# A decoder block on one core: three more weight-sum pieces among the row blocks, two instead of five in the MLP's first product, and an even split of 32 subtractions between VectorE and GpSimd

## The chip, the cores and the metric

The kernel runs on one core of one Trainium2 chip. The metric is device time in microseconds (us) of one execution. The time to beat is the median of three runs. Besides them there is one profiled execution, from which all durations below come.

## The reference, cut to what matters

A block of 2048 tokens by 1024 channels in float32: RMS norm, one projection (queries, keys, values, gMLP inputs, gates), dilated attention and a gated MLP over chunks, two gated branch products, an output product, and a squared-ReLU MLP. The change touches the last two stages:

```python
merged = gate_a * (y_attn @ w_branch_attn) + gate_b * (y_gmlp @ w_branch_gmlp)
y = merged @ w_out
x = x + rmsnorm(y, norm_post_mix)
h = rmsnorm(x, norm_pre_mlp)
a = relu(h @ w_mlp_in)          # 2048 x 1024 by 1024 x 4096
y = (a * a) @ w_mlp_out         # 2048 x 4096 by 4096 x 1024
x = x + rmsnorm(y, norm_post_mlp)
```

## The kernel before, in words

**Precision.** Each float32 operand is split into a high part, rounded to the matmul's format, and a low part, the rest. A product is three matmuls: high by high, high by low, low by high. ScalarE mostly makes the high part; VectorE or GpSimd subtracts to get the low part. On VectorE such a split inside the MLP goes through a copy in PSUM (`staged`), so it needs ScalarE twice and then VectorE.

**The MLP's first product** (`hstep`, `hproduct`, line 1573) uses two levels of a seven-product scheme in place of eight: sums and differences of blocks of the weight and of the input are multiplied, and the products are added up in several places. The outer level has seven phases (`OUTER`): phase 0 uses block A11 of the weight, phase 1 A12, phase 2 the sum S2, phase 3 S1, phase 4 S4, phase 5 S3 and phase 6 A22. Each phase has eight steps q = 0 to 7, and each step seven inner products of six matmuls 128x512. So the stage has 7 x 8 x 7 = 392 products, and this text numbers them from 0 in the order in which TensorE takes them; phase p begins near product 56p. A product's result is read out of PSUM by ScalarE or VectorE and added to the running tiles X.

**Order of the other engines.** In the MLP, ScalarE, VectorE, GpSimd and the DMA queue of SyncE take their instructions exactly as written. After product k, what was put down with `later(k, ...)` is issued, in the order in which it was put down. Each step needs its own inner weight sums (`combine`): five GpSimd operations (lines 1410 to 1416), between ScalarE copies and VectorE reads. GpSimd also makes low parts of the input blocks (`spot`, line 1985), differences of input blocks (lines 1470, 1495), and two kinds of work that the change moves.

**Weight sums.** The phases 2 to 5 need S1 to S4, made once per column block t = 0 to 15 of the weight ("piece") and stored in `wsd`. Pieces below `W_EARLY` are made in part 2, by `w_piece`: two loads of 512 KB into two tiles that exist once, four VectorE operations, two stores issued from GpSimd's queue. The others are made inside the MLP's first product by `w_load`, `w_sum`, `w_store`: four loads, four GpSimd operations, four stores on SyncE's queue. Before, these were five pieces, with loads at products 35, 40, 45 (phase 0) and 122, 126 (phase 2).

**m5.** Phase 3 adds its product M5 into X and also stores it. Phase 5 needs X with M5 in it, phase 6 without. `m5_load` fetches M5 (two tiles of 256 KB for each half f of a step q), and `m5_sub` subtracts it from X, five products later, for the two column halves c = 0, 1.

**Part 2** (merge, `out_block`) runs over four chunks of 512 tokens in the order 2, 3, 0, 1: a merge of 8 column blocks, then four row blocks of 128 tokens. A row block is 48 matmuls; its middle calls `mid`, which lets an older row block do its transposes (`flush_older`). Engines other than TensorE are ordered by the framework here. Half pieces are started by `next_piece`: one call loads, the next one sums and stores, each behind what the engines have in their queues at that point. Calls stand at certain column blocks of the merges and after each row block of the first three chunks.

Of the kernel before, what the change touches and what calls it, by code (L numbers as in the profile page):

```python
# [42 lines left out]
def block_kernel(ctx, tc, a, out):  # L43
    nc = tc.nc
    pe, act, dve, pool, sp = nc.tensor, nc.scalar, nc.vector, nc.gpsimd, nc.sync
# [17 lines left out]
    def psum_mm(name):  # L63
        return ps.tile([P, 512], F32, name=name, tag="mm")

    def psum_aux(name):
        return ps.tile([P, 512], F32, name=name, tag=aux_tag, bufs=BANKS[aux_tag])
# [30 lines left out]
    def mm3(ps, lh, ll, rh, rl, start, stop):  # L98
        pe.matmul(ps, lh, rh, start=start, stop=False)  # L99
        pe.matmul(ps, lh, rl, start=False, stop=False)  # L100
        pe.matmul(ps, ll, rh, start=False, stop=stop)  # L101

    def rstd_of(pl, ss, n, scale, tag):

        r = pl.tile([P, n], F32, name=f"r_{tag}", tag=f"rs_r{n}")
        act.activation(r, ss, AF.Sqrt, bias=eps, scale=scale)  # L106
        v = pl.tile([P, n], F32, name=f"v_{tag}", tag=f"rs_v{n}")
        dve.tensor_scalar(v, ss, scale, EPS, op0=OP.mult, op1=OP.add)
        dve.reciprocal(r, r)  # L109
        t = pl.tile([P, n], F32, name=f"t_{tag}", tag=f"rs_t{n}")  # L110
        if n == 1:
            dve.scalar_tensor_tensor(t, r, v, r, op0=OP.mult, op1=OP.mult)  # L112
        else:
            dve.tensor_mul(t, r, r)
            dve.tensor_mul(t, t, v)
        dve.tensor_scalar(t, t, -0.5, 1.5, op0=OP.mult, op1=OP.add)  # L116
        dve.tensor_mul(r, r, t)  # L117
        return r
# [932 lines left out]
    for n in range(len(units) + 1):  # L1051
        u = None
        if n < len(units):
            g, c, j = units[n]
# [181 lines left out]
    def out_block(c, i, mg, mid):  # L1236

        t0 = c * 512 + i * P
        isl = slice(i * P, (i + 1) * P)
        xt = bot.tile([P, D], F32, name=f"xr_{c}{i}", tag="xr")  # L1240
        sp.dma_start(xt, x[t0:t0 + P, :])
        ss = sm.tile([P, 2], F32, name=f"ss_{c}{i}", tag="ss2")
        pp = [psum_mm(f"o_{c}{i}{n}") for n in range(2)]

        ks = [(n, k) for n in range(2) for k in range(KT)]
        if i == 0:
            ks.remove((0, KT - 1))
            ks.insert(2 * KT - 2, (0, KT - 1))
        for m, (n, k) in enumerate(ks):
            if m == KT:  # L1250
                mid()
            nsl = slice(n * 512, (n + 1) * 512)
            m = mg[k // 4]
            mm3(pp[n], m[:, 0, k % 4, isl], m[:, 1, k % 4, isl], wo[k][:, 0, nsl], wo[k][:, 1, nsl], k == 0, k == KT - 1)
        tt = tt_tile(c, i)
        y1 = bot.tile([P, D], F32, name=f"y1_{c}{i}", tag="y1", bufs=2)
        for n, p in enumerate(pp):
            nsl = slice(n * 512, (n + 1) * 512)
            junk = psum_aux(f"junk_{c}{i}{n}")
            act.activation(junk, p, AF.Square, accum_out=ss[:, n:n + 1])  # L1260
            dve.tensor_mul(y1[:, nsl], p, gpost[:, nsl])
        s1 = sm.tile([P, 1], F32, name=f"s1_{c}{i}", tag="s1")
        dve.tensor_add(s1, ss[:, 0:1], ss[:, 1:2])
        r = rstd_of(sm, s1, 1, 1.0 / D, f"post{c}{i}")
        dve.scalar_tensor_tensor(xt, y1, r, xt, op0=OP.mult, op1=OP.add)
        s2 = sm.tile([P, 1], F32, name=f"s2_{c}{i}", tag="s2")
        act.activation(y1, xt, AF.Square, accum_out=s2)
        pool.dma_start(x1_d[t0:t0 + P, :], xt)
        r2 = rstd_of(sm, s2, 1, 1.0 / D, f"pm{c}{i}")
        dve.scalar_tensor_tensor(y1, xt, r2, gmlp, op0=OP.mult, op1=OP.mult)  # L1270
        yield
        for k in range(0, KT, 4):
            pt = psum_aux(f"pt_{c}{i}{k}")
            for kk in range(4):
                pe.transpose(pt[:, kk * P:(kk + 1) * P], y1[:, (k + kk) * P:(k + kk + 1) * P], ident)
            act.activation(tt[:, k:k + 4], pt.rearrange("p (k t) -> p k t", k=4), AF.Copy)
            pool.dma_start(h2_d[:, k:k + 4, t0:t0 + P], tt[:, k:k + 4])
        yield
# [3 lines left out]
    def flush():  # L1282
        if last:
            next(last.pop(0))

    def flush_older():
        if len(last) > 1:
            flush()
# [18 lines left out]
    def w_piece(t):  # L1307

        w, v = (ttp.tile([P, 2, 512], F32, name=f"{n}w{t}", tag=n, bufs=1) for n in ("tq", "tr"))
        for z, n in ((v, t + NF // 2), (w, t)):  # L1310
# [9 lines left out]
        pool.dma_start(ws_d[q][:, 0:2, f], w)  # L1320
        yield

    W_EARLY = 11
    pieces = deque([w_piece(t) for t in range(W_EARLY - 2)] + [t_piece(0), t_piece(1)] +
                   [w_piece(t) for t in range(W_EARLY - 2, W_EARLY)])
    piece = []
    PIECE_AT = {2: (4, 6), 3: (1, 3, 5, 7), 0: (1, 3, 5, 7), 1: (1, 3, 5, 7)}

    def next_piece():
        with behind():  # L1330
            if piece:
                next(piece.pop(), None)
            elif pieces:
                piece.append(pieces.popleft())
                next(piece[0])

    def merge_pieces(c, dt):
        if dt in PIECE_AT[c]:
            next_piece()
# [31 lines left out]
    NQ, HQ = NF // 2, NF // 4  # L1371
# [54 lines left out]
    def sum_ha(n):  # L1426
        w = hs_[n] = ring(n, f"hs_{n}", [P, 2, 7, 256])
        yield from combine(n, w, hraw_.pop(n))
# [109 lines left out]
    def w_load(t):  # L1538

        outer_t["w", t] = [rx.tile([P, 512], F32, name=f"wt{t}{m}", tag="xs" if (t - W_EARLY) % 2 else "c1", bufs=4) for m in range(4)]  # L1540
        for m, z in enumerate(outer_t["w", t]):
# [58 lines left out]
    m5_ = {}  # L1600
# [6 lines left out]
    def m5_sub(q, f):  # L1607
        for c in range(2):
            x_ = X[2 * q + f][:, c * 512:(c + 1) * 512]
            (dve if q > 3 and not c else pool).tensor_sub(x_, x_, m5_.pop((q, f, c)))  # L1610

    def hstep(k, n, i):

# [49 lines left out]
    def tt_tile(c, i):  # L1663

        w = bot.tile([P, D], F32, name=f"tt{c}{i}", tag=f"yt{i}") if c == 1 else \
            ttp.tile([P, D], F32, name=f"tt{c}{i}", tag="tt")
        return w.rearrange("p (k t) -> p k t", t=P)

    ttp = None
    yt = load_y(2, (("pool", "pool"),) * 4 + (("act", "dve"),) * 2)  # L1670
    early_gates(2)
    mg = merge(2, yt, {}, spatial_out)
    for n, c in enumerate(chunks):
        if n:
            mg = merge(c, yt, {0: flush, 2: flush}, lambda dt: merge_pieces(c, dt))
        for i in range(4):
            b = out_block(c, i, mg, flush_older)
            next(b)
            last.append(b)
            if n < 3 and not i:  # L1680
                yt = load_y(chunks[n + 1])
                for dt, wch in ((0, 0), (0, 1), (1, 0), (1, 1), (2, 0), (2, 1), (3, 0), (3, 1)):
                    with behind():
                        load_gate(chunks[n + 1], dt, wch)
            if n < 3:
                next_piece()
            if n == 3 and i == 1:
                e2r.close()
                egx.close()
                rx = stack(e3, "rx", 1, side="right")  # L1690
                r4 = stack(e3, "r4", 1, side="right")
                for m in range(4):
                    w = r4.tile([P, 2, 512], F32R, name=f"spot{m}", tag=f"spot{m}")
                    spots.append((w[:, 0], w[:, 1]))
                for m in range(2):
                    w = [gtp.tile([P, 512], F32R, name=f"spot{4 + m}{h}", tag=f"gt{m}", bufs=3 - m) for h in range(2)]
                    spots.append(w)
                first_op(0)
                load_ha(0)
                first_op(1)  # L1700
                load_ha(1)
                first_op(2)
                for g in sum_ha(0):
                    pass
                for j in range(2):
                    for kk in range(2):
                        first_split(j, kk)
                for g in sum_ha(1):
                    pass
                for kk in range(2):  # L1710
                    first_split(2, kk)
# [234 lines left out]
    for n in range(8):  # L1946
        t = 2 + 4 * n
        for f, d, args in ((outer_load, 0, ()), (outer_sum, 4, (0,)), (outer_sum, 6, (2,)), (outer_store, 9, ())):
            later(t + d, f, n, *args)
    for n in range(NF // 2 - W_EARLY):  # L1950
        t, d0 = (35, 40, 45, 122, 126)[n], 5 + 2 * (n > 2)
        for f, d, args in ((w_load, 0, ()), (w_sum, d0, (0,)), (w_sum, d0, (1,)), (w_sum, d0 + 1, (2,)),
                           (w_sum, d0 + 2, (3,)), (w_store, d0 + 4, ())):
            later(t + d, f, W_EARLY + n, *args)
    for q in range(HQ):
        t = 7 * 5 * HQ + (20 if q < 4 else 30) + 9 * q
        for f in range(2):
            later(t + 4 * f - 5, m5_load, q, f)
            later(t + 4 * f, m5_sub, q, f)
    gfin = None  # L1960
    for k, (_, stage, n, i) in enumerate(yorder):
# [40 lines left out]
        elif i in (3, ("p", 7)):  # L2002
# [10 lines left out]
            if stage and not more:  # L2013
                f = finish(n)
# [73 lines left out]
```

## Time and profile before

| what | value |
|---|---|
| three runs | 2582.64, 2584.74, 2586.54 us (median 2584.74) |
| the profiled execution | 2587.89 us, of which the span from first to last instruction is 2586.2 us |
| mean granted TensorE clock | 0.994 |
| busy in the span | TensorE 98%, VectorE 66%, ScalarE 49%, GpSimd 54% |
| branch and output products (part 2) | about 1064 to 1401 us |
| MLP, first product | 1401 to 1960 us |
| MLP, second product | 1950 to 2576 us |

In the rows below, PE is TensorE's matmuls, PEld its weight loads, DVE is VectorE, ACT ScalarE, POOL GpSimd, SP the queue of SyncE; L1573 is line 1573 of the kernel. A windows row gives a stretch in us from the span's start, its length, then for PE, PEld, DVE, ACT and POOL the busy time with the number of instructions that were running in the stretch, then the granted clock as a share of full speed, the busy share of the DMA engines and GB/s. A row of waits gives who waited for whom, the total in us, the number of times and the longest. A row of grouped instructions ends with busy us, mean ns, and idle time before them. A timeline row gives start, duration, engine, line, operation, and in brackets the idle time before it and who ended it.

### The profile page before, as it was taken

What the parts mean: (1) busy time and instruction counts of PE and PEld (TensorE: products, weight loads), DVE (VectorE), ACT (ScalarE), POOL (GpSimd) and SP (SyncE); (2) the same over time, 40 slices, a digit from 0 to 9 for tenths busy, and PEclk for the clock granted to TensorE, in tenths of its full rate; (3) what the DMA queues carried; (4) which work ended last, traced back from release to release, by engine and by line L of the source; (5) the groups of instructions that cost most, each with busy time, mean ns of one, the idle gap of its engine ahead of it and who ended that gap; (6) DMA issues with size and microseconds to landing.
All of it is one profiled execution on the core that took longest, in us unless ns stands there. A gap on an engine that the chain in (4) does not pass through costs nothing. (4 is left out here: it accounts for less than half of the span.)

```text
span 2586.2 us, 36297 instructions
## 1 busy us (share of the span) xinstructions
PE 2546.1 (98%) x12122; PEld 2125.5 (82%) x12122; DVE 1695.6 (66%) x3063; ACT 1271.9 (49%) x2696; POOL 1385.4 (54%) x1385
## 2 busy tenths in 40 slices
PE   9999999999999999999999999999999999999998
PEld 8888888888888887788887788888778888888886
DVE  5676575445443447777767678778787777767766
ACT  5213211154446434544445645665447776766755
POOL 0363354274545555311113858787887767767634
PEclk9999999999999999999999999999999999999999
DMA  8779778989897899877766766467884222122235
GB/s 313 284 246 325 254 244 278 308 246 296 264 329 218 239 287 326 279 263 266 272 225 240 249 204 212 145 194 215 259 258 143 90 90 89 51 90 90 90 125 201
DMA packets 413293, 568.73 MB, mean 220 GB/s; under 512 B 58929, under 2 KB 247601, under 8 KB 412082
## 3 DMA queue, kind: packets, MB, share of 16 engines
q1 hardware_dynamic: 387600, 504.73, 59.8%
q0 software_dynamic: 15616, 55.06, 5.6%
q10 hardware_dynamic: 9890, 6.62, 0.8%
q8 instruction: 96, 1.57, 0.3%
q14 instruction: 91, 0.75, 0.1%
HBM read 362.16 MB, written 204.14 MB: 219 GB/s over the span
## 5 line engine op out<-in xcount | busy, mean ns | idle before, releaser
L1573 PE MATMUL ha<-spot,hs 128*128 128x512 f32 x1344 | 327.7, 393 | 8.9 <-ACT hs L1351 2.4
L1883 PE MATMUL ya<-spot,s 128*128 128x512 f32 x1344 | 323.2, 389 | 0.0
L1573 PEld LDWEIGHTS ha<-spot,hs 128*128 128x128 f32 x1344 | 253.5, 189 | 65.6 <-ACT sa L1361 3.3
L1883 PEld LDWEIGHTS ya<-spot,s 128*128 128x128 f32 x1344 | 252.3, 188 | 52.3
L1351 ACT ACTIVATE hs<-hraw 128x512 fp32r<-128x512 f32 x168 | 105.0, 626 | 144.3 <-POOL hraw L1412 123.1
L1573 PE MATMUL hc<-spot,hs 128*128 128x512 f32 x672 | 171.1, 390 | 2.6 <-POOL spot L1985 1.7
L731 PE MATMUL g<-opA,spots 128*128 128x512 f32 x672 | 170.5, 398 | 1.8 <-DVE cv L763 1.8
L1883 PE MATMUL yc<-spot,s 128*128 128x512 f32 x672 | 170.5, 389 | 0.0
L731 PE MATMUL g<-opB,spots 128*128 128x512 f32 x648 | 164.0, 397 | 0.0
L1351 ACT ACTIVATE s<-sraw 128x512 fp32r<-128x512 f32 x168 | 104.2, 620 | 108.2 <-POOL sraw L1412 108.2
L1573 PEld LDWEIGHTS hc<-spot,hs 128*128 128x128 f32 x672 | 126.1, 188 | 30.0 <-POOL spot L1985 2.1
L99 PE MATMUL x<-hT_a,wq 128*128 128x512 f32 x384 | 149.7, 390 | 0.0
L101 PE MATMUL x<-hT_a,wq 128*128 128x512 f32 x384 | 149.5, 389 | 0.0
L100 PE MATMUL x<-hT_a,wq 128*128 128x512 f32 x384 | 149.5, 389 | 0.0
L1883 PEld LDWEIGHTS yc<-spot,s 128*128 128x128 f32 x672 | 126.2, 188 | 26.2
L74 ACT ACTIVATE hl<-r 128x512 fp32r<-128x512 f32 x48 | 30.4, 633 | 236.5 <-POOL r L332 89.0
L731 PEld LDWEIGHTS g<-opA,spots 128*128 128x128 f32 x672 | 121.1, 189 | 23.8 <-issue 2.2
L82 POOL TENSOR_TENSOR spots<-gr,spots 128x512 fp32r<-128x512 f32 x98 | 128.4, 1314 | 22.3 <-DMA gr<-in_w_in_dram 7.9
L1744 ACT ACTIVATE sraw<-sraw 128x1024 f32<-128x1024 f32 x128 | 133.9, 1046 | 2.4 <-DMA sraw<-sd 2.3
L731 PEld LDWEIGHTS g<-opB,spots 128*128 128x128 f32 x648 | 116.9, 189 | 21.1
L76 POOL TENSOR_SCALAR spots<-gr 128x512 fp32r<-128x512 f32 x86 | 55.4, 644 | 131.9 <-PE g L731 97.0
L981 DVE TENSOR_REDUCE o<-po 128x256 f32<-128x512 f32 x48 | 33.2, 692 | 133.9 <-PE po L980 133.9
(471 smaller groups left out, 6844.7 us busy)
## 6 DMA issues: line engine op xcount, KB each, us to landing
sraw<-sd SPq DMA_DIRECT2D x128, 256.0 KB, 3.3
qk<-hl SPq DMA_DIRECT2D x24, 1024.0 KB, 5.7
qq<-qk SPq DMA_DIRECT2D x96, 256.0 KB, 5.4
sd<-e SPq DMA_DIRECT2D x64, 256.0 KB, 3.6
hraw<-wsd SPq DMA_DIRECT2D x32, 512.0 KB, 4.6
w2r<-in_w_mlp_out_dram SPq DMA_DIRECT2D x16, 1024.0 KB, 9.2
g<-gated SPq DMA_DIRECT2D x56, 256.0 KB, 5.5
gr<-sgd SPq DMA_DIRECT2D x53, 256.0 KB, 5.0
```

The lines of the kernel that those rows point to most:

```text
L74: act.activation(hi, src, AF.Copy)
L76: pool.tensor_scalar(hi, src, 1.0, 1.0, op0=OP.mult, op1=OP.mult)
L82: (pool if lo_eng == "pool" else dve).tensor_sub(lo, src, f32(hi))
L99: pe.matmul(ps, lh, rh, start=start, stop=False)
L100: pe.matmul(ps, lh, rl, start=False, stop=False)
L101: pe.matmul(ps, ll, rh, start=False, stop=stop)
L731: pe.matmul(p, w[:, l, k], h[:, r, k], start=i in (1, 6, 5, 4) and not k and not m, stop=k == 3 and m == 2, skip_group_check=True)
L981: dve.tensor_reduce(ot[:, :, j * 64:(j + 1) * 64], po.rearrange("p (b h e) -> p b e h", b=4, h=2), axis=AX.X, op=OP.add)
L1351: act.activation(hi, src, AF.Copy)
L1573: pe.matmul(p, w[:, l, S_AT[i], kk * P:(kk + 1) * P], b[r], start=i in (1, 2, 5) and not kk and not z, stop=kk == 1 and z == 2, skip_group ...
L1744: act.activation(sraw_[n], sraw_[n], func)
L1883: pe.matmul(p, s[:, l], w[r], start=i in (1, 2, 5) and not m and not o, stop=m == 1 and o == 2, skip_group_check=True)
```

## The change

Three pieces more are made in part 2 (`W_EARLY` 14 instead of 11). Their six calls stand in the middle of the second and third row block of the first three chunks (`row_half`). The last two pieces stay in phase 0, with loads at products 35 and 42; phase 2 has none. Of the m5 subtractions, VectorE takes the half c = 0 and GpSimd the half c = 1 of every step; before, VectorE took c = 0 of steps 4 to 7 alone. Their places move: before, products 300 to 331 for steps 0 to 3 and 346 to 377 for steps 4 to 7; now 297 to 308 for steps 0 and 1, and 341 to 380 for steps 2 to 7.

```diff
-    W_EARLY = 11
+    W_EARLY = 14
...
     def m5_sub(q, f):
         for c in range(2):
             x_ = X[2 * q + f][:, c * 512:(c + 1) * 512]
-            (dve if q > 3 and not c else pool).tensor_sub(x_, x_, m5_.pop((q, f, c)))
+            (pool if c else dve).tensor_sub(x_, x_, m5_.pop((q, f, c)))
...
+    def row_half():
+        flush_older()
+        next_piece()
...
-            b = out_block(c, i, mg, flush_older)
+            b = out_block(c, i, mg, row_half if n < 3 and i in (1, 2) else flush_older)
...
     for n in range(NF // 2 - W_EARLY):
-        t, d0 = (35, 40, 45, 122, 126)[n], 5 + 2 * (n > 2)
+        t, d0 = (35, 42)[n], 5
         for f, d, args in ((w_load, 0, ()), (w_sum, d0, (0,)), (w_sum, d0, (1,)), (w_sum, d0 + 1, (2,)),
                            (w_sum, d0 + 2, (3,)), (w_store, d0 + 4, ())):
             later(t + d, f, W_EARLY + n, *args)
     for q in range(HQ):
-        t = 7 * 5 * HQ + (20 if q < 4 else 30) + 9 * q
+        t = 7 * 5 * HQ + (17 if q < 2 else 47) + 7 * q
         for f in range(2):
             later(t + 4 * f - 5, m5_load, q, f)
             later(t + 4 * f, m5_sub, q, f)
```

## Rows read from the trace of the kernel before

**Rows 1.** Windows of 100 us: part 2, MLP first product, MLP second product.
```profile
1200.00:1300.00 100.00, 100.00 (x464) 83.24 (x462) 69.30 (x148) 44.40 (x93) 17.43 (x26) 1.00 0.72 246
1800.00:1900.00 100.00, 94.67 (x407) 76.98 (x406) 72.99 (x113) 44.63 (x87) 77.25 (x80) 0.98 0.81 251
2060.00:2160.00 100.00, 100.00 (x443) 82.83 (x442) 70.06 (x107) 67.17 (x110) 75.34 (x82) 1.00 0.22 75
```

**Rows 2.** Windows closer up, MLP first product.
```profile
1470.00:1500.00 30.00, 25.96 (x105) 20.09 (x104) 18.61 (x29) 20.63 (x41) 28.37 (x29) 0.94 0.66 220
1510.00:1540.00 30.00, 30.00 (x134) 24.86 (x133) 22.48 (x35) 12.60 (x24) 16.46 (x19) 1.00 0.57 168
1605.00:1620.00 15.00, 14.52 (x63) 11.37 (x62) 12.15 (x19) 8.74 (x17) 13.72 (x15) 1.00 0.55 164
1840.00:1890.00 50.00, 44.67 (x187) 35.58 (x186) 35.11 (x55) 27.15 (x53) 48.59 (x48) 0.97 0.67 204
1900.00:1950.00 50.00, 50.00 (x223) 41.28 (x222) 44.65 (x67) 26.66 (x50) 44.03 (x44) 1.00 0.88 270
```

**Rows 3.** Windows of 10 us with waits of PE in them.
```profile
1480.00:1490.00 10.00, 8.07 (x28) 5.94 (x27) 7.23 (x12) 8.13 (x17) 9.76 (x10) 0.84 0.52 188
1880.00:1890.00 10.00, 7.53 (x32) 5.63 (x31) 4.47 (x8) 5.08 (x10) 9.61 (x11) 1.00 0.17 47
```

**Rows 4.** Windows with matmuls and weight loads of line 1573 alone.
```profile
1400.00:1477.00 77.00, 72.50 (x316) 59.09 (x317) 1.00 0.81 281
1400.00:1862.00 462.00, 451.73 (x1971) 370.24 (x1972) 1.00 0.68 219
```

**Rows 5.** Waits of PE, 1402 to 1960 us.
```profile
PE ha L1573 <- ACT hs L1351: 2.4, 1, 2.4
...
PE hc L1573 <- POOL spot L1985: 1.7, 1, 1.7
PE ha L1573 <- ACT X_y L1585: 1.4, 1, 1.4
PE ha L1573 <- POOL spot L1985: 1.3, 1, 1.3
```

**Rows 6.** Waits of ACT, 1855 to 1895 us.
```profile
ACT hs L1351 <- POOL hraw L1412: 19.3, 4, 9.1
```

**Rows 7.** Grouped instructions of POOL, 1840 to 1890 us.
```profile
L1610 POOL TENSOR_TENSOR X_yt<-X_yt,m 128x512 f32<-128x512 f32 x8 | 10.6, 1345 | 0.0
...
L1610 POOL TENSOR_TENSOR X<-X,m 128x512 f32<-128x512 f32 x4 | 5.1, 1294 | 0.0
```

**Rows 8.** Timeline of POOL from 1484 us.
```profile
1484.03 1.30 POOL L1549 TENSOR_TENSOR wt<-wt,wt 128x512 f32<-128x512 f32 x1
1485.29 1.28 POOL L1985 TENSOR_TENSOR spot<-hb,spot 128x512 fp32r<-128x512 f32 x1
```

**Rows 9.** Tile m (M5): durations min/median/max ns, waits, DMA landing.
```profile
L1610 DVE TENSOR_TENSOR X<-X,m x3: 694/1111/1174, 1897.5 to 1909.0; 128x512 f32<-128x512 f32 x3
...
L1610 DVE TENSOR_TENSOR X_y<-X_y,m x2: 911/1220/1530, 1932.2 to 1938.9; 128x512 f32<-128x512 f32 x2
...
DVE X L1610: 4.0, 2
...
DMA to landing us min/median/max: 4.3/6.1/9.2
```

**Rows 10.** Tile of the part-2 pieces: durations min/median/max ns.
```profile
L1315 DVE TENSOR_TENSOR trw<-trw x11: 681/685/692, 1114.3 to 1358.3; 128x512 f32<-128x512 f32 x11
```

**Rows 11.** Timeline of DVE and of PE, fourth row block and next merge.
```profile
1156.85 0.69 DVE L1261 TENSOR_TENSOR y<-o,gpost 128x512 f32<-128x512 f32 x1 [4.26 <-ACT junk L1260]
...
1163.49 1.29 DVE L1270 SCALAR_TENSOR_TENSOR y<-xr,r_pm,gmlp 128x1024 f32<-128x1024 f32 x1
...
1169.07 1.04 PE L1275 MATMUL pt<-ident,y 128*128 128x128 f32 x8
```

**Rows 12.** Waits of PE, 1130 to 1402 us.
```profile
PE pt L1275 <- DVE y L1270: 2.0, 1, 2.0
```

## Prediction

> **What bounds the kernel now.** I read first the windows of 100 us, then closer windows against undisturbed stretches of the same engine, then the waits of TensorE there, and last the queue of the engine that these waits lead to. TensorE is busy without a gap in part 2 and in the MLP's second product [rows 1]; only work on TensorE, or a wait of it, could move the time there, and the change adds no matmul. In the MLP's first product it is not: 1800 to 1900 us held 407 matmuls where 443 fit [rows 1]. An undisturbed 30 us hold 134 and an undisturbed 50 us 223, so 89 take 20 us, 0.225 us each [rows 2]. By that, 1470 to 1500 us lost 134 - 105 = 29 matmuls, 6.5 us (stretch A); 1605 to 1620 us should hold 134 - 15 / 0.225 = 67 and lost 4, 0.9 us (stretch B); 1840 to 1890 us lost 223 - 187 = 36, 8.1 us (stretch C). Together 15.5 us: the purse from which this change can take.
>
> Counting matmuls of line 1573, six to a product, 316 by 1477 us are 52.7 products, and 1971 by 1862 us are 328.5 [rows 4]: A is the end of phase 0 and the beginning of phase 1 (products 48 to 66), C the second half of phase 5. Both are places of the two kinds of work that the diff moves. TensorE's waits there name ScalarE and GpSimd: 2.4 us on `hs` of line 1351 and 1.7 us on `spot` in C, 1.4 us on ScalarE and 1.3 us on `spot` in A [rows 5]. ScalarE itself stood still for GpSimd's line 1412, 19.3 us in four waits, the longest 9.1 us [rows 6]: its queue is in order, so while it waits for a step's weight sums, it reads no product out of PSUM. And GpSimd was busy 28.37 of 30 us in A, 48.59 of 50 us in C [rows 2]. So the bound in A and C is GpSimd's queue.
>
> **The change part by part.**
>
> *Stretch A.* A weight sum is one GpSimd operation of 1.30 us [rows 8], four to a piece, 5.2 us. Before, they are issued after products 40, 40, 41, 42; 45, 45, 46, 47; 50, 50, 51, 52; now the third set is gone and the second stands at 47, 47, 48, 49. The `combine` of products 45 and 46 stood behind two sums of the second piece and now stands ahead of them, 2.6 us earlier; ScalarE's wait for it, and with it TensorE's 1.4 us, should go. The low part that TensorE then waited for (1.3 us) is issued after product 50. Ahead of it were two sums of the third piece, the second at 1484.03 us, and it ran from 1485.29 us, to 1486.57 us [rows 8]. With two sums fewer it ends 2.6 us earlier; but TensorE, no longer held before, comes some 2.3 us earlier too (1.4 us and smaller waits). So this wait stays, about 1.3 us. The granted clock in 1480 to 1490 us was 0.84 on the mean, with a stretch at 1.2 GHz after the three waits [rows 3]; in 1880 to 1890 us, with a wait of 1.7 us among 2.5 us of idle, it stayed at 1.00, 2.4 GHz [rows 3, 5]. I take the latter for the one wait that stays. Gain 6.5 - 1.3 = 5.2 us; bounds 6.5 (the wait goes too) and 2 (the clock falls after all: 10 us at 0.84 cost 1.6 us, and a longer wait).
>
> *Stretch B.* The two pieces of phase 2 go, 8 sums, 10.4 us of GpSimd before 1605 us, where it was busy 13.72 of 15 us [rows 2, 8]. Gain 0.9 us; bounds 0 and 0.9.
>
> *Stretch C.* Twelve of GpSimd's m5 subtractions ran in it, 10.6 + 5.1 = 15.7 us of its 48.6 [rows 7]. Now products 309 to 340 have none; GpSimd's four of steps 0 and 1 run at 297 to 308, in front of C, where eight ran (products 300 to 313). GpSimd then has some 33 of 50 us in C, and the line 1412 that ScalarE waited for comes up to 9 us earlier. Gain 8.1 us; bounds 8.1 and 4, if what I add in front of it takes half.
>
> *What it adds in front of C.* VectorE gets four subtractions within 12 products (16 us). On VectorE one took 0.69 to 1.53 us, with medians of 1.1 and 1.2 [rows 9]; I take 1.0, so 4 us, beside the differences of input blocks that fall there too. TensorE needs each PSUM bank again four products later, 5.4 us, less the product itself and VectorE's read of 0.7 us: VectorE may be some 3 us late. I take 0.7 us; bounds 0 and 3.
>
> *What it adds in phase 6.* Each engine gets 12 subtractions at products 341 to 380 instead of 8 at 346 to 377: every 3.5 products instead of 4.5. In 50 us (37 products) that is 10.6 instead of 8.2, 2.4 more; VectorE goes from 44.65 to some 47 us, GpSimd at 1.35 us each from 44.03 to 47.3 us [rows 2, 7, 9]. Tight, but not over. Behind each subtraction wait VectorE's reads of PSUM, and behind those TensorE. I take 0.8 us; bounds 0 and 4. In the rows, VectorE's subtraction took 0.69 us alone, and up to 1.53 us where GpSimd does the other half of the same tile just then [rows 9]. The Trainium skill (GPSIMD Engine Reference, section 1, Specifications) says that GpSimd shares its SBUF interfaces with VectorE and contends with VectorE instructions that have two SBUF inputs, which is what `m5_sub` issues, now always to both engines at once; the trace agrees with that. If each of VectorE's took the longest time, 10.6 x 1.53 - 8.2 x 1.0 = 8 us come on top of 44.65 in 50 us: VectorE is the bound by 2.7 us, and the sum loses 2 to 3 us more. This is inside the bound of 4.
>
> *Part 2.* Three pieces: 12 VectorE operations of 0.685 us are 8.2 us; 6 stores on GpSimd's queue; 6 loads of 512 KB on SyncE's queue [rows 10]. TensorE is full there, and VectorE has 69 of 100 us, GpSimd 17 [rows 1], so the cover is there. The sums now also stand between two row blocks' chains on VectorE. What hangs behind them is the normalised row block, which TensorE transposes later: for the fourth row block it was ready at 1164.8 us and taken at 1169.07 us, 4.3 us in hand, and before the fourth's reads VectorE stood idle for 4.26 us, which takes up 2.74 us of sums [rows 11]. The loads must wait on SyncE's queue for the stores of the piece before (the tiles exist once), and the next rows of x queue behind; these wait for the x tile's own store anyway. Without that cover, the one such wait in the trace cost 2.0 us [rows 12]. I take 0.8 us for three chunks; bounds 0 and 6. The transformed input pieces, `t_piece`, come one row block later and are read only in the fourth chunk; that costs nothing.
>
> *Sum.* 5.2 + 0.9 + 8.1 - 0.7 - 0.8 - 0.8 = 11.9 us. The profiled execution, 2587.89 us, would become 2576.0 us. It lies 3.15 us over the median of the three runs; taken from that median: 2584.74 - 11.9 = 2572.8, so 2573 us.
>
> **Rivals.** Under 0.2% (5.2 us) a measurement of this kernel can't be told from no change.
>
> *VectorE and DMA take GpSimd's place, in part.* A keeps its low clock (gain 2), C keeps half (4), the three costs come to 2 us: 2584.7 - 4 = 2581; with one of the three mended, 2578. For it: VectorE is at 89% in phase 6. Against: it is not behind in C, where it waits itself.
>
> *GpSimd wasn't it.* The waits of A and C name ScalarE as often as GpSimd [rows 5]; were ScalarE's own order the cause, no stall would move: 2585 us. Against: its waits for line 1412 [rows 6].
>
> *Slower.* Late M5 loads in phase 6. Each subtraction comes 5 products (6.8 us) after its load was issued. Loads landed in 6.1 us, at most 9.2 us; VectorE stood 4.0 us in two waits for them, 2.0 us each, and TensorE lost nothing [rows 9]. Now there are 12 pairs instead of 8, on DMA engines that were 88% busy in 1900 to 1950 us [rows 2]. It decides from about 10 us of landing, where VectorE's 3 us in hand are gone. At 11.5 us each of the 12 costs some 1.7 us: 2584.7 - 14.2 + 1.5 + 20 = 2592 us. Against: in C SyncE's queue was held up by GpSimd's backlog, and the loads then came in a bunch; without it they spread out.
>
> *Part 2 stalls.* At each of three chunks the transposes wait 2.0 us and the clock then falls once (1.6 us): 10.8 us lost instead of 0.8, 2583 us.
>
> **How the numbers follow.** The forecast, 2569 to 2577 us, has a chance of 0.62; VectorE and DMA in part 0.17; no effect 0.08; late loads 0.08; part 2 0.05. Faster by over 0.2% means under 2579.6: all of the first and two thirds of the second, with a little of the rest: 0.74. Slower is the late loads: 0.08. The remainder, 0.18, is the same. The low end of the range is the whole purse without a cost, 2584.7 - 15.5 = 2569, less 1 for the spread of runs: 2568; the high end takes the second case with all its costs: 2582.
>
> **What would show it.** In A, GpSimd with some 5 us less and one wait of TensorE left, on `spot`, at the clock of 2.4 GHz; in B none; in C 220 or more matmuls in 50 us and no long wait of ScalarE for line 1412; in phase 6 VectorE some 94% busy, and windows there still full. Wrong it would be through windows of phase 6 under 215 matmuls in 50 us, with VectorE waiting for m5's DMA, or through TensorE waiting for line 1270 in the merges of part 2.

## The result and the profile after

The changed kernel takes 2589.2 us in the median of 16 runs (2585.8 to 2600.52), the kernel before, measured beside it, 2584.28 us (2580.12 to 2588.22): a ratio of 1.0019 with a 95% interval of [1.0012, 1.0026], 4.9 us slower where 11.9 us less were forecast. The two profiled executions don't show this sum: that of after took 2586.54 us, that of before 2587.89 us. They show where the change acts.

Three starts cut the time at the two borders that matter: the last weight load of the row sums (line 551) begins part 2, the first matmul of line 1573 ends it and begins the MLP's first product, the last one ends that. Operations grouped by line, before and then after; the columns are count, min/median/max in ns, first and last start:

```profile
L551 PEld LDWEIGHTS rowsum<-wsp,ones x4: 187/188/188, 473.3 to 1052.5; 128*128 128x128 f32 x4
L1573 PE MATMUL ha<-spot,hs x1344: 387/389/662, 1401.4 to 1958.4; 128*128 128x512 f32 x192
L1573 PE MATMUL hc<-spot,hs x672: 387/389/505, 1415.5 to 1959.7; 128*128 128x512 f32 x168
```

```profile
L551 PEld LDWEIGHTS rowsum<-wsp,ones x4: 187/188/188, 471.8 to 1049.8; 128*128 128x128 f32 x4
L1573 PE MATMUL ha<-spot,hs x1344: 387/389/504, 1412.6 to 1956.9; 128*128 128x512 f32 x192
L1573 PE MATMUL hc<-spot,hs x672: 389/389/499, 1426.6 to 1958.2; 128*128 128x512 f32 x168
```

Part 2 went from 1401.4 - 1052.5 = 348.9 us to 362.8 us, 13.9 us more. The first product went from 1959.7 - 1401.4 = 558.3 us to 545.6 us, 12.7 us less. So the gain that the prediction worked out is there, and a loss of the same size stands in front of it.

The gain, in windows of stretches A, B, C and phase 6, moved by what part 2 and the stalls shift them (against [rows 2]):

```profile
1482.00:1512.00 30.00, 28.46 (x126) 23.13 (x125) 22.68 (x36) 23.14 (x46) 25.51 (x28) 1.00 0.65 216
1616.00:1631.00 15.00, 15.00 (x68) 12.43 (x67) 12.35 (x20) 7.29 (x14) 13.30 (x14) 1.00 0.14 37
1846.00:1896.00 50.00, 49.67 (x220) 40.79 (x219) 43.78 (x68) 31.01 (x60) 41.57 (x44) 1.00 0.73 222
1896.00:1946.00 50.00, 50.00 (x222) 41.39 (x221) 45.95 (x68) 25.39 (x48) 44.28 (x45) 1.00 0.89 290
```

A holds 126 matmuls instead of 105, C 220 instead of 187, B and phase 6 are full. The clock stays at 1.00, 2.4 GHz, in all four.

The loss, in the waits of TensorE in part 2, 1090 to 1412 us (against [rows 12]), and of VectorE there, 1115 to 1380 us, after; columns: us in total, times, longest:

```profile
PE b L99 <- DVE g L1211: 8.0, 3, 3.1
PE pt L1275 <- DVE y L1270: 4.5, 5, 2.0
```

```profile
DVE trw L1315 <- DMA trw<-in_w_mlp_in_dram: 23.1, 6, 5.5
DVE xr L1265 <- DMA xr<-in_x_dram: 20.9, 6, 4.4
...
DVE trw L1316 <- DMA tqw<-in_w_mlp_in_dram: 6.8, 4, 2.7
```

The 2.0 us among the waits for line 1270 is the old one. The others are new: 8.0 us for VectorE's reads of PSUM in the merges (line 1211) and 2.5 us for row blocks not normalised in time. VectorE itself stands for pieces and for rows of x; in the kernel before the same three rows, in the same window, read:

```profile
DVE trw L1315 <- DMA trw<-in_w_mlp_in_dram: 5.6, 2, 4.4
DVE trw L1316 <- DMA tqw<-in_w_mlp_in_dram: 5.0, 2, 2.7
...
DVE xr L1265 <- DMA xr<-in_x_dram: 2.6, 2, 1.6
```

How the first of them comes about, VectorE's timeline in the first chunk's first row blocks, after; in brackets the idle time and what ended it:

```profile
1122.26 0.16 DVE L108 TENSOR_SCALAR v_post<-s 128x1 f32<-128x1 f32 x1
1127.00 0.69 DVE L1315 TENSOR_TENSOR trw<-trw 128x512 f32<-128x512 f32 x1 [4.58 <-DMA trw<-in_w_mlp_in_dram]
1127.61 0.16 DVE L109 RECIPROCAL r_post<-r_post 128x1 f32<-128x1 f32 x1
...
1130.23 1.28 DVE L1265 SCALAR_TENSOR_TENSOR xr<-y,r_post,xr 128x1024 f32<-128x1024 f32 x1
...
1140.54 1.28 DVE L1265 SCALAR_TENSOR_TENSOR xr<-y,r_post,xr 128x1024 f32<-128x1024 f32 x1 [3.53 <-DMA xr<-in_x_dram]
```

The piece's sums stand between lines 108 and 109, in the middle of a row block's chain. VectorE's queue is in order: it stands 4.58 us for the piece, with the chain half done. Line 1265, which completes x, comes later, so does the store of the x tile, and as that tile exists once, the next rows of x are loaded later and VectorE waits for them, 3.53 us. In all it waits six times for x, 20.9 us; what these waits cost by themselves comes up with e8 below. In the merge behind these row blocks, VectorE then stands for the next piece in front of line 1211:

```profile
1180.18 0.69 DVE L1315 TENSOR_TENSOR trw<-trw 128x512 f32<-128x512 f32 x1 [1.98 <-DMA trw<-in_w_mlp_in_dram]
1183.38 0.69 DVE L1316 TENSOR_TENSOR trw<-tqw,trw 128x512 f32<-128x512 f32 x1 [2.50 <-DMA tqw<-in_w_mlp_in_dram]
1183.99 0.68 DVE L1211 TENSOR_TENSOR g<-g,b 128x512 f32<-128x512 f32 x1
```

TensorE, which needs that PSUM bank again, stood still with it, and in the second such merge the clock fell (window of 15 us; 40 matmuls where [rows 1] have 464 in 100 us, so 70):

```profile
1262.00:1277.00 15.00, 11.87 (x40) 9.21 (x40) 9.32 (x16) 4.65 (x9) 1.43 (x2) 0.77 0.75 279
```

Thirty matmuls of 0.2155 us are 6.5 us, 3.1 of them the wait and 3.4 the clock at its lower level, 1.2 GHz. The sum, 8.0 + 2.5 + 3.4 = 13.9 us, is what part 2 lost, but that it fits to the tenth is chance. The kernel before had a fall of the clock of its own in part 2, at the old wait of 2.0 us for line 1270; after had none at that wait (before, then after):

```profile
1380.00:1390.00 10.00, 9.30 (x38) 7.86 (x39) 6.87 (x18) 4.03 (x11) 2.11 (x3) 0.83 0.40 154
1390.00:1400.00 10.00, 8.01 (x40) 6.50 (x39) 6.77 (x15) 4.74 (x12) 2.69 (x4) 1.00 0.34 121
```

10 us at 0.83 cost 1.7 us, so these rows explain 12.2 us, and 1.7 us have no row. The whole of part 2, before and after:

```profile
1052.50:1401.40 348.90, 341.91 (x1576) 282.47 (x1574) 252.68 (x483) 160.62 (x323) 78.48 (x97) 0.99 0.71 245
1049.80:1412.60 362.80, 345.60 (x1577) 282.67 (x1575) 258.25 (x496) 160.55 (x323) 82.72 (x103) 0.99 0.72 252
```

TensorE stood 7.0 us in it before and 17.2 us after: 10.2 of the 13.9 us are idle time.

### The profile page after: what moved, and what is told of

The parts are those of the page before. It is cut to its first block, busy times and chain, and to the rows that moved or that the text cites. A ratio compares the mean times of both kernels' runs of the same rounds, so it can differ in the third digit from the quotient of the medians.

```text
span 2584.8 us, 36269 instructions
## 1 busy us (share of the span) xinstructions
PE 2542.6 (98%) x12122; PEld 2121.6 (82%) x12122; DVE 1705.8 (66%) x3083; ACT 1272.4 (49%) x2696; POOL 1368.0 (53%) x1371
```

## The experiments

Theory 1: VectorE waits in order for a piece's load, amid the chain and in the merges. Theory 2: VectorE has no room for 8 us more. Theory 3: six more loads and stores take the DMA's time. Part 2 and the first product are cut as above, from each kernel's profiled execution; these lie from 3.6 us below to 6.5 us above the medians. The kernels in which part 2 is unchanged (before, e1, e9, e10, e7) have 345.6 to 351.4 us, and the changed kernel and e2, which share one part 2, 362.8 and 368.0, so a difference of under 6 us of part 2 is not read. Kernels measured together share one set of runs of before; ratios go by that set.

| kernel | median us | ratio to before, 95% | part 2, us | first product, us |
|---|---|---|---|---|
| changed kernel | 2589.20 | 1.0019 [1.0012, 1.0026] | 362.8 | 545.6 |
| e1 m5 alone | 2579.61 | 0.9979 [0.9971, 0.9988] | 348.3 | 553.0 |
| e2 pieces alone | 2596.66 | 1.0048 [1.0033, 1.0062] | 368.0 | 551.7 |
| e9 m5, engines alone | 2580.53 | 0.9979 [0.9969, 0.9988] | 347.0 | 554.2 |
| e10 m5, places alone | 2581.28 | 0.9989 [0.9980, 0.9998] | 345.6 | 553.1 |
| e3 calls behind the rows | 2579.47 | 0.9978 [0.9967, 0.9988] | 358.7 | 545.7 |
| e4 loads amid rows left out | 2577.76 | 0.9973 [0.9964, 0.9982] | 353.8 | 545.8 |
| e8 sums amid rows left out | 2576.67 | 0.9965 [0.9953, 0.9978] | 350.2 | 547.5 |
| e6 those sums on GpSimd | 2591.49 | 1.0025 [1.0012, 1.0037] | 365.5 | 546.1 |
| e13 later in the merges | 2585.24 | 0.9989 [0.9980, 0.9998] | 362.3 | 545.6 |
| e11 both, e3 and e13 | 2569.99 | 0.9939 [0.9925, 0.9952] | 345.0 | 548.4 |
| e15 e1 and e13, no extra piece | 2576.29 | 0.9968 [0.9956, 0.9980] | 347.0 | 554.1 |
| e7 three pieces in phase 2 | 2579.70 | 0.9982 [0.9974, 0.9991] | 351.4 | 553.6 |
| e12 one piece in part 2 | 2578.42 | 0.9971 [0.9961, 0.9981] | 350.4 | 550.1 |
| e14 e11, piece at 40 | 2571.41 | 0.9954 [0.9941, 0.9967] | 343.0 | 548.0 |

**The two halves.** e1 is the kernel before with m5's two edits, e2 the changed kernel without them.

```diff
-            (dve if q > 3 and not c else pool).tensor_sub(x_, x_, m5_.pop((q, f, c)))
+            (pool if c else dve).tensor_sub(x_, x_, m5_.pop((q, f, c)))
-        t = 7 * 5 * HQ + (20 if q < 4 else 30) + 9 * q
+        t = 7 * 5 * HQ + (17 if q < 2 else 47) + 7 * q
```

> Before with the new places and engines of the m5 subtractions alone; part 2 and the five pieces of weight sums in the MLP stay. Theory 1 (late load: the changed kernel loses in part 2, because the sums amid a row block wait on VectorE for their load, and gains in the MLP as forecast): stretch C mended, A and B as before, part 2 as before: 2584.3 - 7.0 = 2577 us. Rival (C was mended because phase 2's sums went, not by m5): no change, 2584 us.

> The changed kernel with the m5 subtractions as before: only the pieces move. Theory 1: part 2 loses its 14 us, A and B give 5 to 6 back, C stays: 2584.3 + 14 - 5.5 = 2593 us. Rival (the loss of part 2 in the profile is that one execution's): 2584.3 - 5.5 = 2579 us.

m5 alone gains 0.21%, and 5.3 us in the first product, 2.6 us short of its forecast by the median; the pieces alone lose 0.48%, 3.7 us more than forecast, with a part 2 of 368.0 us. The loss belongs to the pieces.

**m5's two edits apart.** e9 takes the first of the two lines above, e10 the second.

> The kernel before, with m5's subtractions shared evenly between the two engines from the first on, at the places that they had. Of the twelve that GpSimd had in stretch C it keeps six, 7.8 us less of its 48.6 of 50. If the stall of C is GpSimd's load there, half of it or more goes: 2579 to 2581 us. If it is the places, nothing moves: 2584 us.

> The kernel before, with m5's subtractions at the new places and by the engines that they had: GpSimd does all of the first four steps' and half of the rest. Stretch C holds none of them and loses nothing; but eight of GpSimd's stand in 297 to 308, and sixteen in phase 6, 21 us of GpSimd more than the eight before over some 53 us that had 6 us free. If the load of GpSimd is what makes TensorE wait, the stall moves to phase 6 and the time is 2582 to 2590 us; if the places alone mend it, 2579 us.

Each alone gives nearly all that both give in the first product, 4.1 and 5.2 of 5.3 us: C stalled because GpSimd was full there, and six subtractions fewer were enough. The places alone didn't move the stall to phase 6: in 1893 to 1943 us GpSimd was busy 47.27 of 50 us, and TensorE held 222 matmuls. Of the sixteen subtractions that e10's forecast counts there, eight had stood there before, so GpSimd got 10.4 us more and not 21. By the whole time e10 can't be told from e1.

**What in part 2 costs it.** e3 keeps all work and traffic and moves the six extra calls from amid the row blocks to behind them. e4 keeps the places, but fills the tiles of the pieces begun behind the first and second row block instead of loading them.

```diff
-            b = out_block(c, i, mg, row_half if n < 3 and i in (1, 2) else flush_older)
+            b = out_block(c, i, mg, flush_older)
...
             if n < 3:
                 next_piece()
+                if i in (1, 2):
+                    next_piece()
```

```diff
+            if filled[0]:
+                pool.memset(z, 0.01)
+            else:
                 sp.dma_start(z.rearrange("p a c -> p (a c)"), a["w_mlp_in"][n].rearrange("p k c -> p (k c)"))
...
+                filled[0] = i in (0, 1)
                 next_piece()
+                filled[0] = False
```

> The changed kernel with the six extra calls moved from the middle of the second and third row block to the end of the same row block, so that a piece's sums come behind the row block's whole chain, a row block after its load; work and traffic are the same. Theory 1 (late load): the waits of TensorE in part 2 all but go, 2584.3 - 12.6 + 2 = 2574 us. Theory 2 (VectorE has no room for 8 us more of work in part 2): as the changed kernel, 2589 us. Theory 3 (6 MB more of DMA traffic): 2589 us.

> The changed kernel, but the pieces that are loaded after the first and second row block of the first three chunks are filled by GpSimd with a constant instead of loaded (so part of the weight is not computed with); sums, stores and their places stay. Theory 1 (late load): VectorE no longer waits in the chain, part 2 loses under 4 us: 2584.3 - 12.6 + 4 = 2576 us or less. Theory 2 (VectorE's work): 2589 us. Theory 3 (traffic): two thirds of the loss stay, 2585 us.

Both are faster than before, e4 1.8 us and e3 5.5 us short of what theory 1 gave. Theory 2 has e4 against it, which has all of VectorE's sums, and theory 3 has the time of e3, which has all transfers (its part 2 isn't told from the changed kernel's). e8 leaves the sums amid the row blocks out and keeps the loads and stores, e6 does these sums on GpSimd.

```diff
-        dve.tensor_add(a22, a21, a22)          # this one and the next three
+        if not amid[0]:                        # e8
+            dve.tensor_add(a22, a21, a22)
+        e = pool if amid[0] else dve           # e6
+        e.tensor_add(a22, a21, a22)
```

> The changed kernel without the sums of the pieces that end inside a row block (24 of VectorE's operations are left out, so these weight sums are stored as they were loaded); their loads and stores stay, the stores now waiting for the load by themselves. Theory 1 (VectorE stands in the middle of a row block's chain until a piece's load lands, and with it the x tile's store and its next load): part 2 comes to 351 to 355 us and the time to 2574 to 2578 us, though all the transfers of the change are there. Theory 3 (the six loads and stores more): part 2 stays at 361 to 363 us, 2589 us.

> The changed kernel, with every step of a piece that starts from inside a row block told to do its sums on GpSimd instead of VectorE; loads, stores, places and tiles stay as they are. Theory 1 (VectorE's queue is in order and stands for a piece's load in the middle of a row block's chain): the 4.6 us wait of VectorE amid the chain goes, the chains keep the times that they had before, and part 2 comes back from 362.8 us to about 350 to 353 us, the time to 2574 to 2577 us. Theory 3 (six more loads and six more stores take the DMA's time): nothing changes, 2589 us. A third way, found since: what hurts is that the next piece's tiles come free late, in the merge, because they exist once; GpSimd's sums take 5.2 us a piece instead of 2.7, so this would stay or grow: the waits for line 1211 in the merges stay, 2585 to 2589 us.

(One of the six pieces that end amid a row block is a `t_piece`, whose sums stay on VectorE in both: 20 operations are left out or moved, not 24.) e8 has every transfer of the change, and part 2 is back at 350.2 us: theory 3 falls for good. In it TensorE keeps one wait for line 1211, 4.2 us, in the last merge. e6 missed theory 1's number, and shows why that theory was told too narrowly. The third way of its forecast came about: TensorE's waits for line 1211 in the merges stay and grow (1090 to 1417 us):

```profile
PE b L99 <- DVE g L1211: 11.0, 5, 3.5
```

The row blocks' chains are held up in other ways. GpSimd's timeline in e6, where lines from 1315 on stand one lower, and VectorE's for the same block and the next:

```profile
1145.66 1.28 POOL L1317 TENSOR_TENSOR trw<-tqw,trw 128x512 f32<-128x512 f32 x1 [0.98 <-DMA tqw<-in_w_mlp_in_dram]
...
1149.47 2.17 POOL L1320 TENSOR_TENSOR tqw<-tqw 128x512 f32<-128x512 f32 x1
1152.05 0.73 POOL L1321 DMA_DIRECT2D wsd<-tqw  x1 [0.41 <-POOL tqw L1320]
1152.78 0.57 POOL L1268 DMA_DIRECT2D x1d<-xr  x1
```

```profile
1145.71 1.25 DVE L117 TENSOR_TENSOR r_post<-r_post,t_post 128x1 f32<-128x1 f32 x1
...
1148.52 1.97 DVE L1265 SCALAR_TENSOR_TENSOR xr<-y,r_post,xr 128x1024 f32<-128x1024 f32 x1 [1.55 <-DMA xr<-in_x_dram]
...
1162.45 1.28 DVE L1265 SCALAR_TENSOR_TENSOR xr<-y,r_post,xr 128x1024 f32<-128x1024 f32 x1 [4.62 <-DMA xr<-in_x_dram]
```

Line 1265 had x ready at 1148.52 + 1.97 = 1150.5 us, but its store stood behind the piece's sums and stores in GpSimd's queue until 1152.78 us, 2.3 us late, and VectorE stood 4.62 us for the next rows of x. The wait for a piece amid the chain was gone from VectorE, and the x tile's round (sum, store, load) was held up in another queue. Besides, VectorE's operations took longer beside GpSimd's sums: line 117 took 1.25 us instead of some 0.15 and ended with line 1317, line 1265 took 1.97 instead of 1.28. So e6 does not part these ways.

What a late round of x costs by itself is not shown. VectorE's waits for x, 1115 to 1380 us, in e1, whose part 2 is that of the kernel before, and in e8:

```profile
DVE xr L1265 <- DMA xr<-in_x_dram: 9.7, 5, 3.2
```

```profile
DVE xr L1265 <- DMA xr<-in_x_dram: 15.3, 8, 4.1
```

Both have more of them than the kernel before (2.6 us), and still a part 2 of 348.3 and 350.2 us.

**The merges.** e3 kept four waits for line 1211, 7.6 us together; VectorE stood there for the piece that the merge itself starts. In e13 the changed kernel does the sums of that piece one column block later, in e11 e3 does, in e15 e1 does.

```diff
-    PIECE_AT = {2: (4, 6), 3: (1, 3, 5, 7), 0: (1, 3, 5, 7), 1: (1, 3, 5, 7)}
+    PIECE_AT = {2: (4, 6), 3: (1, 4, 5, 7), 0: (1, 4, 5, 7), 1: (1, 4, 5, 7)}
```

> The version with the extra calls behind the row blocks, whose part 2 still took 358.7 us, with one more edit: in the merges of the last three chunks the first piece's sums are issued behind the fifth column block instead of the fourth, 4 us later, so that the load has landed when VectorE comes to them. There VectorE stood 2.2 + 2.8, 3.5 + 1.8 and 5.7 us for those loads, and TensorE 2.8, 0.8 and 3.8 us for VectorE's line 1211. Theory 1, told of the merges too: these three stalls go or shrink to under 1 us each, part 2 comes to 352 us, the time to 2573 to 2576 us. If the second piece of the merge, which now has only the time from its load to the merge's end, takes the wait over: 2579 to 2581 us.

> The changed kernel with the six calls where it has them, amid the row blocks, and with the later sums in the merges (fifth column block instead of fourth). If what hurts is mostly the merges, where TensorE stood 2.2, 3.1 and 2.7 us for line 1211 and ran 6.8 us at half clock, those go and the time is 2577 to 2580 us; the four short waits for line 1270, 2.5 us together, stay. If the wait amid the chain makes everything behind it late whatever the merges do (theory 1 in its first form), the merges' loads still land too late: TensorE keeps two or three of the waits for line 1211, and the time is 2584 to 2588 us. With the calls behind the rows and the same edit it was 2570.0 us.

> The kernel before with m5 as the change has it and the later sums in the merges, but no more pieces in part 2 than the kernel before has. It tells what of the 2570.0 us is owed to the extra pieces. m5 alone was 2579.6 us, part 2 348.3 us with one wait of 2.3 us for line 1211. If the late loads in the merges are the extra pieces' doing alone, the edit is worth 2 us here: 2577 to 2578 us, so the three pieces are worth 7 to 8 us once they don't wait. If the merges lost more than that before, it is 2573 to 2575 us and the pieces are worth 3 to 5 us.

The waits of TensorE in part 2, 1090 to 1390 us, in e3, in e11, and to 1400 us in e13:

```profile
PE b L99 <- DVE g L1211: 7.6, 4, 3.6
PE pt L1275 <- DVE y L1270: 2.0, 1, 2.0
```

```profile
PE pt L1275 <- DVE y L1270: 1.3, 1, 1.3
PE b L99 <- DVE gates L1211: 0.5, 1, 0.5
```

```profile
PE pt L1275 <- DVE y L1270: 9.6, 6, 2.7
PE b L99 <- DVE g L1211: 1.5, 2, 0.8
```

e11 has no wait for `g` of line 1211 left, and of those for line 1270 only the old one, now 1.3 us. By its median it is the fastest kernel of the study (e14 is not told from it), 0.6% under before and 3 us under the range forecast for it. It has all of VectorE's sums and all transfers of the change, so theories 2 and 3 fall with it as well. In e13 the waits for line 1211 shrink to 1.5 us, but those for line 1270 grow from 4.5 to 9.6: the chain that stood still in the row block is late at its transposes instead. So its time lies in the second range of its forecast, but not by the waits named there. e13 and e11 differ by nothing but the place of six calls: 0.9989 - 0.9939 = 0.50%, 13 us. e15 against e1 has the merge edit alone, 0.11%, which the intervals don't tell apart from nothing; and e11 against e15 has the three pieces, moved from the MLP phases to part 2: worth 0.9968 - 0.9939 = 0.29%, some 7 us, once TensorE no longer waits for them. Amid the chain, the changed kernel against e1, they cost 1.0019 - 0.9979 = 0.40%; behind the rows without the merge edit, e3 against e1, they gain nothing that the intervals show (0.01%).

**Other places.** e7 does the three pieces in phase 2 instead, e12 only one of them in part 2, behind the first chunk's rows. The lines shown hold the numbers that they change; neither has calls amid the row blocks.

```diff
-    W_EARLY = 14
+    W_EARLY = 11                                          # e7; 12 in e12
-        t, d0 = (35, 42)[n], 5
+        t, d0 = (35, 42, 118, 124, 130)[n], 5 + 2 * (n > 1)   # e7
+        t, d0 = (35, 42, 122, 126)[n], 5 + 2 * (n > 1)        # e12
```

> The changed kernel without its three more pieces in part 2: they are done in the third MLP phase instead, on GpSimd, from products 118, 124 and 130; the two pieces at 35 and 42 and m5's new places and engines stay. Part 2 should take 349 us again, as in the kernel before. Stretches A and C keep what the change gave them, 3.5 and 8 us. The third phase has twelve sums, 15.6 us of GpSimd, where the kernel before had eight and lost 0.9 us: 1 to 3 us lost. Theory 1 and its rivals all give 2573 to 2575 us; over 2578 us would say that A or C needed something else of the change, or that the third phase can't carry three pieces.

> One piece more in part 2 instead of three, its calls behind the second and third row block of the first chunk; two pieces in the third MLP phase, where the kernel before has them (products 122 and 126), two at 35 and 42, m5 as in the changed kernel. Stretches A and C as after the change, 3.5 and 8 us gained, B as before, part 2 at 349 to 352 us: 2574 to 2577 us. If each extra piece costs its share of what three cost in that version (10 us of part 2, 3.3 each) it is 2577 us; if one costs as much as three, 2582 us.

Phase 2 can't carry three: TensorE waited 3.9 us once and the clock fell, and the first product lost some 8 us against the changed kernel. e12 still had one merge wait of 2.8 us, and its time is 1.4 us over its forecast. Neither is told from e1: in e7, with a first product of 553.6 us, what A gains is given back.

**The wait left in A.** e14 is e11 with `(35, 40)` for `(35, 42)`.

> The version with the calls behind the row blocks and the later sums in the merges (2570.0 us), with the second piece of the first MLP phase at product 40 instead of 42. There one wait of TensorE was left in stretch A, 1.7 us at product 56; it stood on VectorE's line 1587, and that for the store of the piece's tile, whose buffer the first stage tile of the next phase takes over. If the store is the cause, it comes two products, 2.7 us, earlier, the wait goes, and the time is 2568 to 2569 us. If the low part (spot) that the prediction named is the cause, nothing moves, 2570 us. Against both, the piece's sums at 45 to 47 stand ahead of the combines of products 45 and 46 again, which cost 1.4 us in the kernel before: 2569 to 2571 us.

The wait for line 1587 went, the 1.4 us for the combine that the prediction had read in [rows 5] came back, and the time is that of e11 or 1.4 us more: the third way.

## Why the prediction was wrong

**The purse and stretches A, B, C: right.** 5.2 + 0.9 + 8.1 - 0.7 - 0.8 = 12.7 us were forecast for the first product, and 12.7 us is what the two profiles show. That they agree to the tenth is luck: by the windows A gained 126 - 105 = 21 matmuls, 4.7 us, and C 33, 7.4 us, 1.2 us less together than forecast, and the costs were smaller too. A kept one wait at full clock, B none, C has 220 matmuls, and ScalarE's longest wait for line 1412 there fell from 9.1 [rows 6] to 4.2 us. e9 and e10 confirm GpSimd's load as the cause in C, and e14 the combine's as one in A.

**A's remaining wait: right in size, wrong in name.** It was to be 1.3 us on `spot`; it was 1.5 us, on line 1587. VectorE's timeline:

```profile
1493.66 0.69 DVE L1587 TENSOR_TENSOR e<-X_yt,ha 128x512 f32<-128x512 f32 x1 [2.16 <-DMA wsd<-wt]
```

The stage tile of the first product of phase 1 takes over a buffer of the second piece, and waited for that piece's store.

**In front of C and phase 6: right.** TensorE lost 0.6 us at product 308 (0.7 forecast); phase 6 has 222 matmuls in 50 us with VectorE at 45.95 us. M5's loads landed in 4.0 to 8.2 us and no wait of TensorE names them, so the forecast's slower rival didn't happen. VectorE's subtractions took 0.68 to 1.84 us. The Trainium skill (GPSIMD Engine Reference, section 1, Specifications) says that GpSimd contends with VectorE instructions that have two SBUF inputs. The trace agrees: the longest of them, 1.84 us, started at 1940.23 us together with GpSimd's. Windows of phase 6 stayed full all the same.

**Part 2: the step that failed.** It was 0.8 us with an upper bound of 6, and measured 13.9. Its sum took VectorE's free time for cover and had no term for VectorE's wait for a piece's load, neither amid a row block's chain nor in the merges, where line 1211 cost 8.0 us. The kernel before already had such waits, 10.6 us in four (above). "TensorE is full there" was read from one window of 100 us; over the whole of part 2 it stood 7.0 us. Two sentences were wrong, and a third looked past something. The sums were put "between two row blocks' chains"; they stand inside the first one's. The cover was measured in work, 2.74 us of sums in an idle time of 4.26 us; what VectorE spent was a wait for a load, 4.58 us. It was set by when the tile came free (the store of the piece before was issued at 1113.14 us and landed 7.0 us later, the load was issued at 1120.11 us) and by the load's 6.8 us to landing, and not by how long the sums take. And that the rows of x "wait for the x tile's own store anyway" looked past a wait that grew, VectorE's for x from 2.6 to 20.9 us; by e8 it is open what that costs by itself. With the calls behind the rows, the merges alone are worth 0.9978 - 0.9939 = 0.39% (e3 against e11). The rival "Part 2 stalls" had a loss of 10.8 us and a chance of 0.05; it had the place, TensorE in the merges, but named line 1270, where 2.5 us were lost, and not line 1211 with 8.0.

The medians differ by 4.9 us, the profiled part 2 and first product together by 13.9 - 12.7 = 1.2 us. Single executions scatter by more than this. The changed kernel and e2, with one and the same part 2, have 365.4 us on the mean, the five kernels with the part 2 of before 348.2 us: a loss of 17.2 us by this estimate, and 17.2 - 12.7 = 4.5 us. The granted clock, too, varies from run to run: the 16 runs of the changed kernel have means from 0.992 to 0.997, and the time goes with them, by some 2 us for 0.001 (2600.52 us at 0.992, 2585.8 at 0.997). The profile of before had 0.994 and lay 3.6 us over the median of its runs, that of after had 0.996 and lay 2.7 us under. Why the clock falls in one run and not in another stays open.

## What to carry to other kernels

Work that waits for a load costs, on an in-order queue, its wait and not its duration: before inserting it, read when its load lands there, and which chain it would cut. Look for such waits in the kernel as it is, at every place where the same tiles are filled: here the merges had them as well as the row blocks, and mending one of the two was not enough. Where an engine has room, place such work where a chain ends and as late as the next use allows: the same three pieces cost 0.40% amid the chain, change nothing behind it, and gain 0.29% behind it with the sums in the merges later too.

## What was not expected of the hardware

TensorE's clock did not fall with every wait: after the 3.1 us in the second merge it ran at its lower level (0.77 over 15 us, above), after waits of 2.2 and 2.7 us in the first and third it stayed at 1.00 in the 10 us windows of these waits and the ones behind them; at the wait of 2.0 us for line 1270 it fell in before and not in after (above). The windows of the first and the third:

```profile
1180.00:1190.00 10.00, 7.82 (x35) 6.14 (x34) 7.18 (x12) 3.80 (x7) 1.43 (x2) 1.00 0.76 278
...
1350.00:1360.00 10.00, 7.33 (x33) 5.71 (x31) 6.26 (x11) 2.51 (x5) 1.43 (x2) 1.00 0.71 261
```
